# A retention decoder on one core: 32x32 block turns and small transfers in place of transposes on TensorE

## The chip, the cores and the metric

The kernel runs on one core of one Trainium2 chip. The metric is the device time of one execution in microseconds (us), as the median of several runs; lower is better. The profile is of one execution.

## The reference, cut to what matters

One decoder layer over 272 tokens (16 learned meta tokens ahead of 256) with 2048 channels. One input projection of width 22,528 feeds a conformer branch (gated linear unit, causal depthwise convolution of 31 taps, layer norm) and a retention branch of 8 heads; two gates merge them, an output projection and a final norm follow.

```python
qf = rotate_pairs(q, cos, sin) * (RET_QK_DIM ** -0.5)
kf = rotate_pairs(k, cos, sin)
o = retention_chunkwise(qf, kf, v)          # per head: (q k^T * decay) v, 256 x 512 out
o = head_groupnorm(o, ret_gn_w[l], ret_gn_b[l])
y_b = (o * jax.nn.silu(ret_gate)) @ ret_out[l]
merged = jax.nn.sigmoid(merge_a) * y_a + jax.nn.sigmoid(merge_b) * y_b
h_res = h_res + merged @ w_out[l]
```

All data is float32.

## The kernel before, in words

The weights are streamed as chunks of 1 MB (128 x 2048 float32). `seq` is the list of chunks with the work of each; the loop at L731 goes through it. In step i it issues the load of chunk i+3 on SP's queue (three buffers `raw`), splits chunk i+2 into a high and a low part (`cut`: ACT copies `raw` to `whi` rounded to fp32r, VectorE subtracts to give `wlo`; three buffers of each), runs the functions that `marks` holds for step i, then some convolution taps from the list `bg` (VectorE), then the chunk's matmuls and the copies out of PSUM. Each product is made of three fp32r products, high x high, high x low and low x high. Activations lie with channels on the partitions and tokens along the row (`hn`), so a projected chunk comes out as 128 channels x 272 (`project`, L204) or 256 tokens (`project_wide`, L214).

The source order is not the order on the engines: the framework keeps each engine's instructions in one compiled order, and places an instruction where its operands are expected to be ready; the engines then run that order, each waiting on semaphores.

Chunks of one head, in order (before): 2 gates of the linear unit (`sig_b`), 2 of its values (`glu`, after which the head's convolution taps join `bg`), for every head but the first the 4 output-product chunks of the head before (`ret_out_chunks(h - 1)`), 2 of q, 2 of k, 4 of v (`val` copies each from PSUM to `s["v"]`), 4 of the retention gate. That is 20 chunks a head, 16 for the first.

A head's retention runs at marks, counted from the head's first chunk (for heads 1 to 7; four less for head 0):

- `scores` at 14: k by q products on TensorE, times the decay.
- `values` at 17: the values have channels on the partitions, but the next product needs tokens there. Eight 128x128 transposes on TensorE (L394) write two PSUM banks; ACT and VectorE split them into `vhi`, `vlo`. Four more transposes (L402) turn copies of the last 32 tokens. Copies of rows 0 to 31 (`pe`, `ve`) prepare an edge product.
- `attend` at 19: eleven matmuls of 512 columns; group-norm statistics on VectorE, a power -0.5 on POOL (L103), then ACT writes the normalised output `on` (tokens on the partitions).
- `gated` at 21, which is chunk 1 of the next head: eight transposes on TensorE (L454) turn `on` back to channels on the partitions; ACT applies the group norm's scale and shift into `z`, VectorE multiplies by the gate, and `z` is split into `zhi`, `zlo`, which the output products read from chunk 4 of the next head.

The pool `ret` has one buffer for each tag, so tiles of one tag follow each other in one place: `on`; `vT` (the values, then `z`); `zhi`; `zlo`.

The last head's output products come behind four chunks of the merge gate; then follow the rest of the merge gate, the conformer's gate and output, and the output projection.

Of the kernel before, what the change touches and what calls it, by code (L numbers as in the profile page):

```python
# [10 lines left out]
F32 = mybir.dt.float32  # L11
# [5 lines left out]
P = 128  # L17
# [3 lines left out]
SEQ = 256  # L21
# [3 lines left out]
HEADS = 8  # L25
# [11 lines left out]
def hybrid_kernel(ctx: ExitStack, tc, xt, xrow, xnat, par, fg, cs, dec, win, cout, rout, wout, out):  # L37
    nc = tc.nc
# [7 lines left out]
    def bank(pool=misc):  # L46
        return pool.tile([P, 512], F32, tag="ps", name="ps")
# [36 lines left out]
    ident = pers.tile([P, P], F32, name="ident")  # L84
# [168 lines left out]
        stream(win[blk], use)  # L253

    bg = []


    ret = None
# [18 lines left out]
    def head(h):  # L277
        s = {}
        st[h] = s

        def sig_b(j):
            def f(acc):
                t = ret.tile([P, L], F32, tag="sgb", name="sgb", bufs=2)
                s["b", j] = t
                nc.vector.tensor_tensor(out=t, in0=acc[:, 0:L], in1=row, op=ALU.mult)
                nc.scalar.activation(out=t, in_=t, func=AF.Sigmoid)
                nc.vector.tensor_tensor(out=t, in0=t, in1=row, op=ALU.mult)
            return f

        def glu(j):  # L290
            def f(acc):
                nc.vector.tensor_tensor(out=u_sb[j][:, PAD:], in0=acc[:, 0:L], in1=s["b", j], op=ALU.mult)
                if j == 1:
                    bg.extend(conv_ops(h))
            return f

        def rot(which, j, n):
            def f(acc):
                t = ret.tile([P, 2, n], F32, tag=f"rt{j}", name=f"rt{j}")
                s[which, j] = t  # L300
                if n == SEQ:
                    x = tmp.tile([P, SEQ], F32, tag="sg", name="sg")
                    halves(acc, x)
                    acc = x
                nc.vector.tensor_tensor(out=t, in0=acc[:, 0:n].unsqueeze(1).broadcast_to([P, 2, n]),
                                        in1=cs_sb[:, :, L - n:], op=ALU.mult)
                if j == 1:
                    t0, t1 = s[which, 0], t
                    r = ret.tile([P, 2, n], F32, tag=which + "r", name=which + "r")
                    nc.vector.tensor_tensor(out=r[:, 0], in0=t0[:, 0], in1=t1[:, 1], op=ALU.subtract)  # L310
                    nc.vector.tensor_tensor(out=r[:, 1], in0=t1[:, 0], in1=t0[:, 1], op=ALU.add)
                    hi = ret.tile([P, 2, n], F32R, tag=which + "hi", name=which + "hi")
                    lo = ret.tile([P, 2, n], F32R, tag=which + "lo", name=which + "lo")
                    split(r, hi, lo)
                    s[which] = (r, hi, lo)
            return f

        def val(j):
            def f(acc):
                if j == 0:  # L320
                    s["v"] = ret.tile([P, 4, L], F32, tag="vT", name="vT")
                nc.scalar.copy(out=s["v"][:, j], in_=acc[:, 0:L])
            return f

        def gate(j):
            def f(acc):
                if j == 0:
                    s["g"] = ret.tile([P, 4, SEQ], F32, tag="gs", name="gs")
                g, t = s["g"][:, j], tmp.tile([P, SEQ], F32, tag="sg", name="sg")
                halves(acc, g)  # L330
                nc.vector.tensor_tensor(out=g, in0=g, in1=row[:, NMETA:], op=ALU.mult)
                nc.scalar.activation(out=t, in_=g, func=AF.Sigmoid)
                nc.vector.tensor_tensor(out=g, in0=g, in1=t, op=ALU.mult)
            return f

        for j in range(2):
            proj_chunk(B0 + 2 * h + j, L, sig_b(j))
        for j in range(2):
            proj_chunk(A0 + 2 * h + j, L, glu(j))
        if h:  # L340
            ret_out_chunks(h - 1)
        for j in range(2):
            proj_chunk(Q0 + 2 * h + j, SEQ, rot("q", j, SEQ))
        for j in range(2):
            proj_chunk(K0 + 2 * h + j, L, rot("k", j, L))
        for j in range(4):
            proj_chunk(V0 + 4 * h + j, L, val(j))
        for j in range(4):
            proj_chunk(R0 + 4 * h + j, SEQ, gate(j))

    def scores(h):
# [32 lines left out]
        nc.scalar.activation(out=ph, in_=p2, func=AF.Copy)  # L384
        nc.vector.tensor_tensor(out=ph[64:96], in0=p2[64:96], in1=ph[64:96].bitcast(F32), op=ALU.subtract)

    def values(h):
        s = st[h]
        v = s["v"]
        s["vn"] = []  # L390
        for j in range(2):
            ps = bank()
            for b in range(4):
                nc.tensor.transpose(ps[:, b * P:(b + 1) * P], v[:, b, j * P:(j + 1) * P], ident)  # L394
            hi = ret.tile([P, DV], F32R, tag=f"vhi{j}", name=f"vhi{j}")
            lo = ret.tile([P, DV], F32R, tag=f"vlo{j}", name=f"vlo{j}")
            split(ps, hi, lo)
            s["vn"].append((hi, lo))
        ps = bank()
        last = last32(ret, v, 4)  # L400
        for b in range(4):
            nc.tensor.transpose(ps[0:96, b * P:(b + 1) * P], last[:, b], ident)  # L402
        v2 = ret.tile([96, DV], F32R, tag="v2", name="v2")
        nc.scalar.activation(out=v2, in_=ps[0:96], func=AF.Copy)
        nc.vector.tensor_tensor(out=v2[32:64], in0=ps[32:64], in1=v2[32:64].bitcast(F32), op=ALU.subtract)
        s["v2"] = v2

        pe = ret.tile([96, P], F32R, tag="qr", name="pe")
        ve = ret.tile([96, DV], F32R, tag="kr", name="ve")
        for n, (a, b) in enumerate(((0, 0), (0, 1), (1, 0))):  # L410
            rows = slice(32 * n, 32 * n + 32)
            nc.scalar.copy(out=pe[rows], in_=s["p"][a][0:32, SEQ:SEQ + P].bitcast(F32))
            nc.scalar.copy(out=ve[rows], in_=s["vn"][1][b][0:32].bitcast(F32))
        s["edge"] = (pe, ve)

    def attend(h):
# [24 lines left out]
        for i in range(2):  # L441
            nc.scalar.activation(out=on[:, i], in_=pss[i], func=AF.Identity, scale=rs[:, i:i + 1],
                                 bias=sh[:, i:i + 1])

    def gated(h):
        s = st[h]
        z = ret.tile([P, 4, SEQ], F32, tag="vT", name="z")
        for pair in range(2):
            ps = bank()
            for b in range(2):  # L450
                for i in range(2):
                    o = b * SEQ + i * P
                    vb = 2 * pair + b
                    nc.tensor.transpose(ps[:, o:o + P], s["on"][:, i, vb * P:(vb + 1) * P], ident)  # L454
            for b in range(2):
                vb = 2 * pair + b
                nc.scalar.activation(out=z[:, vb], in_=ps[:, b * SEQ:(b + 1) * SEQ], func=AF.Identity,
                                     scale=pcol(C_GW, 4 * h + vb), bias=pcol(C_GB, 4 * h + vb))
        nc.vector.tensor_tensor(out=z, in0=z, in1=s["g"], op=ALU.mult)
        hi = ret.tile([P, 4, SEQ], F32R, tag="zhi", name="zhi")  # L460
        lo = ret.tile([P, 4, SEQ], F32R, tag="zlo", name="zlo")
        split(z, hi, lo)
        s["z"] = (hi, lo)

    def ret_out_chunks(h):
        for g in range(4):
            def use(hi, lo, g=g):
                z_hi, z_lo = st[h]["z"]
                hi = hi.rearrange("p (k c) -> p k c", k=4)
                lo = lo.rearrange("p (k c) -> p k c", k=4)  # L470
                for half in range(2):
                    acc = bank(accp)
                    for b in range(2):
                        col = (2 * half + b) * P
                        contract(acc[:, b * SEQ:(b + 1) * SEQ], hi, lo, z_hi, z_lo, range(4), slice(col, col + P))
                    y = yb[:, 4 * g + 2 * half:4 * g + 2 * half + 2]
                    a = acc.rearrange("p (b t) -> p b t", b=2)
                    if h == 0:
                        nc.scalar.copy(out=y, in_=a)
                    else:  # L480
                        nc.vector.tensor_tensor(out=y, in0=a, in1=y, op=ALU.add)
            stream(rout[4 * h + g], use)
# [4 lines left out]
    for h in range(HEADS):  # L487
        base = len(seq)
        head(h)
        ex = 4 if h else 0  # L490
        marks.setdefault(base + 10 + ex, []).append(lambda h=h: scores(h))
        marks.setdefault(base + 13 + ex, []).append(lambda h=h: values(h))
        marks.setdefault(base + 15 + ex, []).append(lambda h=h: attend(h))
        marks.setdefault(base + 17 + ex, []).append(lambda h=h: gated(h))


    fin = {}
# [328 lines left out]
```

## Time and profile before

| | us |
|---|---|
| median of 3 runs (lowest to highest) | 1459.52 (1456.3 to 1460.04) |
| the profiled execution | 1456.36 |
| span of its instructions | 1454.5 |
| TensorE busy (matmuls) | 1439.5 |
| VectorE busy | 1070.4 |
| ACT busy | 688.3 |
| POOL busy | 10.8 |

The span runs from the first to the last instruction; the time of the execution lies 1.9 us above it. Busy time of TensorE counts each matmul from its start to its modelled end, so neighbouring matmuls overlap in it: what one costs in a row of many is read from start to start. The granted TensorE clock is at its full level, 2.4 GHz, over the whole span (0.999 of it). The other engines have idle time, which costs nothing unless TensorE waits for them.

### The profile page before, as it was taken

What the parts mean: (1) busy time and instruction counts of PE and PEld (TensorE: products, weight loads), DVE (VectorE), ACT (ScalarE), POOL (GpSimd) and SP (SyncE); (2) the same over time, 40 slices, a digit from 0 to 9 for tenths busy, and PEclk for the clock granted to TensorE, in tenths of its full rate; (3) what the DMA queues carried; (4) which work ended last, traced back from release to release, by engine and by line L of the source; (5) the groups of instructions that cost most, each with busy time, mean ns of one, the idle gap of its engine ahead of it and who ended that gap; (6) DMA issues with size and microseconds to landing.
All of it is one profiled execution on the core that took longest, in us unless ns stands there. A gap on an engine that the chain in (4) does not pass through costs nothing.

```text
span 1454.5 us, 23167 instructions
## 1 busy us (share of the span) xinstructions
PE 1439.5 (99%) x9808; PEld 1338.5 (92%) x9808; DVE 1070.4 (74%) x1467; ACT 688.3 (47%) x834; POOL 10.8 (1%) x27
## 2 busy tenths in 40 slices
PE   8999999999999999999999999999999999999997
PEld 8999999999999999999999999989888888888886
DVE  5797946985895796698589569767878876666553
ACT  6555445345444534634443553454555654444433
POOL 0000000000000000000000000000000000000000
PEclk9999999999999999999999999999999999999999
DMA  8655554554554545455445545545455555555752
GB/s 328 228 181 175 174 182 160 179 191 145 178 196 157 174 174 184 172 174 178 173 154 198 165 164 175 186 160 177 171 203 177 200 177 198 176 196 180 289 177 84
DMA packets 39527, 265.74 MB, mean 183 GB/s; under 512 B 4448, under 2 KB 4448, under 8 KB 8416
## 3 DMA queue, kind: packets, MB, share of 16 engines
q1 hardware_dynamic: 37776, 258.70, 51.5%
q10 hardware_dynamic: 1584, 5.57, 1.0%
q8 instruction: 77, 1.26, 0.3%
q14 instruction: 26, 0.21, 0.0%
q0 software_dynamic: 64, 0.00, 0.0%
HBM read 262.15 MB, written 2.10 MB: 182 GB/s over the span
## 4 chain that ended last, share of the span: by engine, by line
PE 99%; issue 0%; ACT 0%; DMA 0%; DVE 0%; POOLq 0%; POOL 0%
PE ps L222 29%; PE ps L220 15%; PE ps L208 11%; PE ps L209 11%; PE ps L211 11%; PE ps L237 4%; PE ps L234 4%; PE ps L235 4%; PE ps L614 2%; PE ps L617 2%; PE ps L613 2%; PE ps L454 0%; PE ps L394 0%; PE ps L430 0%; PE ps L429 0%
## 5 line engine op out<-in xcount | busy, mean ns | idle before, releaser
L51 DVE TENSOR_TENSOR wlo<-raw,whi 128x2048 fp32r<-128x2048 f32 (+1 forms) x246 | 549.9, 2236 | 177.8 <-ACT whi L50 151.1
L50 ACT ACTIVATE whi<-raw 128x2048 fp32r<-128x2048 f32 (+1 forms) x246 | 461.0, 1875 | 304.9 <-PE ps L209 125.7
L222 PE MATMUL ps<-hn,whi 128*128 128x512 f32 x1536 | 384.4, 397 | 0.0
L222 PEld LDWEIGHTS ps<-hn,whi 128*128 128x128 f32 x1536 | 285.4, 189 | 59.0
L208 PE MATMUL ps<-hn,whi 128*128 128x272 f32 x1280 | 326.4, 290 | 7.2 <-ACT whi L50 5.3
L209 PE MATMUL ps<-hn,whi 128*128 128x272 f32 x1280 | 324.9, 287 | 0.0
L208 PEld LDWEIGHTS ps<-hn,whi 128*128 128x128 f32 x1280 | 241.1, 188 | 7.5 <-ACT whi L50 5.3
L209 PEld LDWEIGHTS ps<-hn,whi 128*128 128x128 f32 x1280 | 241.2, 188 | 0.9 <-DVE hn L156 0.2
L272 DVE SCALAR_TENSOR_TENSOR c_sb<-u,par_sb,c_sb 128x256 f32<-128x256 f32 x480 | 205.9, 477 | 1.5
L220 PEld LDWEIGHTS ps<-hn,wlo 128*128 128x128 f32 x1536 | 194.8, 189 | 8.9
L220 PE MATMUL ps<-hn,wlo 128*128 128x256 f32 x1536 | 197.1, 282 | 0.0
L211 PE MATMUL ps<-hn,wlo 128*128 128x272 f32 x1280 | 172.9, 287 | 0.0
L227 ACT COPY half<-ps 128x256 f32<-128x256 f32 x112 | 41.7, 372 | 276.4 <-PE ps L222 276.2
L211 PEld LDWEIGHTS ps<-hn,wlo 128*128 128x128 f32 x1280 | 164.6, 188 | 0.0
L234 PE MATMUL ps<-zhi,whi 128*128 128x256 f32 x512 | 125.9, 280 | 0.0
L235 PE MATMUL ps<-zlo,whi 128*128 128x256 f32 x512 | 125.9, 280 | 0.0
L234 PEld LDWEIGHTS ps<-zhi,whi 128*128 128x128 f32 x512 | 96.3, 188 | 0.0
L235 PEld LDWEIGHTS ps<-zlo,whi 128*128 128x128 f32 x512 | 96.2, 188 | 0.0
L237 PE MATMUL ps<-zhi,wlo 128*128 128x256 f32 x512 | 80.9, 280 | 0.0
L237 PEld LDWEIGHTS ps<-zhi,wlo 128*128 128x128 f32 x512 | 69.1, 188 | 0.0
L222 PE MATMUL ps<-s,whi 128*128 128x512 f32 x256 | 64.7, 395 | 0.0
L222 PEld LDWEIGHTS ps<-s,whi 128*128 128x128 f32 x256 | 47.9, 188 | 10.2
(164 smaller groups left out, 1041.5 us busy)
## 6 DMA issues: line engine op xcount, KB each, us to landing
raw<-in_win_dram SPq DMA_DIRECT2D x174, 1024.0 KB, 4.9
raw<-in_rout_dram SPq DMA_DIRECT2D x32, 1024.0 KB, 4.9
raw<-in_cout_dram SPq DMA_DIRECT2D x16, 1024.0 KB, 4.9
raw<-in_wout_dram SPq DMA_DIRECT2D x16, 1024.0 KB, 4.8
dec<-in_dec_dram ACTq DMA_DIRECT2D x8, 264.0 KB, 4.0
raw<-in_win_dram SPq DMA_DIRECT2D x8, 256.0 KB, 6.8
xr<-in_xrow_dram SPq DMA_DIRECT2D x2, 1024.0 KB, 10.2
tail<-in_xnat_dram ACTq DMA_DIRECT2D x1, 2048.0 KB, 8.5
```

The source lines that it names most:

```text
L50: nc.scalar.activation(out=hi, in_=src, func=AF.Copy)
L51: nc.vector.tensor_tensor(out=lo, in0=src, in1=hi.bitcast(F32), op=ALU.subtract)
L208: nc.tensor.matmul(acc[:, 0:L], lhsT=w, rhs=hn_hi[:, k], start=(k == 0), stop=False)
L209: nc.tensor.matmul(acc[:, 0:L], lhsT=w, rhs=hn_lo[:, k], start=False, stop=False)
L211: nc.tensor.matmul(acc[:, 0:L], lhsT=lo[:, k * P:(k + 1) * P], rhs=hn_hi[:, k], start=False, stop=(k == KT - 1))
L220: nc.tensor.matmul(acc[:, 0:SEQ], lhsT=lo[:, j * P:(j + 1) * P], rhs=a[:, j, 0], start=False, stop=False)
L222: nc.tensor.matmul(both, lhsT=hi[:, k * P:(k + 1) * P], rhs=a[:, k], start=(k == 0), stop=(k == KT - 1))
L227: nc.scalar.copy(out=t, in_=acc[:, SEQ:])
L234: nc.tensor.matmul(acc, lhsT=hi[:, k, col], rhs=a_hi[:, k], start=(j == 0), stop=False)
L235: nc.tensor.matmul(acc, lhsT=hi[:, k, col], rhs=a_lo[:, k], start=False, stop=False)
L237: nc.tensor.matmul(acc, lhsT=lo[:, k, col], rhs=a_hi[:, k], start=False, stop=(j == n - 1))
L272: nc.vector.scalar_tensor_tensor(out=c, in0=u[:, t:t + SEQ], scalar=w, in1=c, op0=ALU.mult, op1=ALU.add)
```

## The change

For heads 0 to 6 the transposes of the values and of the retention output leave TensorE. Each becomes two steps. VectorE turns every 32x32 block in place of partitions (`nc.vector.transpose`, two instructions of 128x512 for each). Then sixteen transfers, issued on POOL's queue, carry the blocks between the four groups of 32 partitions: transfer (a, q) reads 32 partitions x 1 KB and writes 32 partitions x 8 runs of 128 B. ACT and VectorE then read the turned data from the tiles `vy` and `oy` instead of from PSUM. The last head stays as it was.

The marks of those heads move: the new `turn_values` stands at 17, `values` at 20 (before 17), `attend` at 21 (before 19), the new `turn_out` at 23, `gated` at 26 (before 21); 20 and more are chunks 0 and more of the next head. The output products of head h-1 move behind q and k of head h, from chunks 4 to 7 to chunks 8 to 11, for every head from 1 on. New tiles share the tags of old ones: the block-turned values `vx` and later `z` take `on`, `vy` takes `zhi`, `ox` takes `vT`, `oy` takes `zlo`.

```diff
     bg = []
+    BY_PE = (HEADS - 1,)
...
-        if h:
-            ret_out_chunks(h - 1)
         for j in range(2):
             proj_chunk(Q0 + 2 * h + j, SEQ, rot("q", j, SEQ))
         for j in range(2):
             proj_chunk(K0 + 2 * h + j, L, rot("k", j, L))
+        if h:
+            ret_out_chunks(h - 1)
...
+    def blocks_moved(src, dst):
+
+        for a in range(4):
+            for q in range(4):
+                nc.gpsimd.dma_start(out=dst(q, a), in_=src(q, a))
+
+    def turn_values(h):
+
+        s = st[h]
+        if h in BY_PE:
+            return
+        x = ret.tile([P, 4, 2, 4, 32], F32, tag="on", name="vx")
+        for j in range(2):
+            nc.vector.transpose(out=x[:, :, j].rearrange("p q b t -> p b q t"),
+                                in_=s["v"][:, :, j * P:(j + 1) * P].rearrange("p b (q t) -> p b q t", q=4))
+        y = s["vy"] = ret.tile([P, 2, 4, P], F32, tag="zhi", name="vy")
+        blocks_moved(lambda q, a: x[32 * a:32 * a + 32, q].rearrange("p j b t -> p (j b) t"),
+                     lambda q, a: y[32 * q:32 * q + 32, :, :, 32 * a:32 * a + 32].rearrange("p j b t -> p (j b) t"))
...
         for j in range(2):
-            ps = bank()
-            for b in range(4):
-                nc.tensor.transpose(ps[:, b * P:(b + 1) * P], v[:, b, j * P:(j + 1) * P], ident)
+            if h in BY_PE:
...
+            else:
+                ps = s["vy"][:, j].rearrange("p b t -> p (b t)")
...
+    def turn_out(h):
+
+        s = st[h]
+        if h in BY_PE:
+            return
+        x = ret.tile([P, 4, 4, 2, 32], F32, tag="vT", name="ox")
+        for i in range(2):
+            nc.vector.transpose(out=x[:, :, :, i].rearrange("p q b t -> p b q t"),
+                                in_=s["on"][:, i].rearrange("p (b q t) -> p b q t", b=4, q=4))
+        y = s["oy"] = ret.tile([P, 4, SEQ], F32, tag="zlo", name="oy")
+        ys = y.rearrange("p b (i t) -> p (b i) t", i=2)
+        blocks_moved(lambda q, a: x[32 * a:32 * a + 32, q].rearrange("p b i t -> p (b i) t"),
+                     lambda q, a: ys[32 * q:32 * q + 32, :, 32 * a:32 * a + 32])
...
-        z = ret.tile([P, 4, SEQ], F32, tag="vT", name="z")
+        z = ret.tile([P, 4, SEQ], F32, tag="vT" if h in BY_PE else "on", name="z")
...
+            else:
+                ps = s["oy"][:, 2 * pair:2 * pair + 2].rearrange("p b t -> p (b t)")
...
-        marks.setdefault(base + 10 + ex, []).append(lambda h=h: scores(h))
-        marks.setdefault(base + 13 + ex, []).append(lambda h=h: values(h))
-        marks.setdefault(base + 15 + ex, []).append(lambda h=h: attend(h))
-        marks.setdefault(base + 17 + ex, []).append(lambda h=h: gated(h))
+        late = h not in BY_PE
+        for at, f in ((10, scores), (13, turn_values), (16 if late else 13, values), (17 if late else 15, attend),
+                      (19, turn_out), (22 if late else 17, gated)):
+            marks.setdefault(base + at + ex, []).append(lambda h=h, f=f: f(h))
```

## Rows read from the trace of the kernel before

**Rows 1.** The page, part 1: busy us (share), instructions, by engine.

```profile
PE 1439.5 (99%) x9808; PEld 1338.5 (92%) x9808; DVE 1070.4 (74%) x1467; ACT 688.3 (47%) x834; POOL 10.8 (1%) x27
```

**Rows 2.** Waits of TensorE, whole run: us in total, times, longest us.

```profile
PE ps L208 <- ACT whi L50: 5.3, 1, 5.3
PE ps L208 <- DVE sgb L285: 1.9, 1, 1.9
```

**Rows 3.** Timeline of TensorE, second head: start us, us, engine, line, instructions.

```profile
214.90 0.40 PE L222 MATMUL ps<-hn,whi 128*128 128x512 f32 x1
215.14 1.03 PE L394 MATMUL ps<-ident,vT 128*128 128x128 f32 x8
216.01 0.60 PE L402 MATMUL ps<-ident,last 128*96 128x128 f32 x4
216.36 3.80 PE L222 MATMUL ps<-hn,whi 128*128 128x512 f32 x15
...
227.74 0.39 PE L429 MATMUL ps<-vhi,phi 128*128 128x512 f32 x1
...
230.29 3.69 PE L222 MATMUL ps<-hn,whi 128*128 128x512 f32 x15
...
235.94 0.28 PE L208 MATMUL ps<-hn,whi 128*128 128x272 f32 x1
236.06 0.29 PE L209 MATMUL ps<-hn,whi 128*128 128x272 f32 x1
...
241.91 1.03 PE L454 MATMUL ps<-ident,on 128*128 128x128 f32 x8
242.71 0.37 PE L208 MATMUL ps<-hn,whi 128*128 128x272 f32 x1
242.92 0.29 PE L209 MATMUL ps<-hn,whi 128*128 128x272 f32 x1
```

**Rows 4.** Groups of instructions by shape: busy us, mean ns of one, idle before.

```profile
L305 DVE TENSOR_TENSOR rt<-sg,cs_sb 128x512 f32<-128x512 f32 x16 | 10.8, 683 | 0.0
L394 PE MATMUL ps<-ident,vT 128*128 128x128 f32 x64 | 8.3, 272 | 0.0
```

**Rows 5.** Timeline of VectorE, second head (in brackets: idle before, releaser).

```profile
215.74 0.42 DVE L228 TENSOR_TENSOR gs<-ps,half 128x256 f32<-128x256 f32 x1 [3.70 <-ACT half L227]
...
247.37 1.23 DVE L51 TENSOR_TENSOR zlo<-z,zhi 128x1024 fp32r<-128x1024 f32 x1 [1.13 <-ACT zhi L50]
```

**Rows 6.** Busy us of each engine in one head's stretch, clock, DMA share, GB/s.

```profile
331.00:454.00 123.00, 123.00 (x915) 118.17 (x914) 94.68 (x134) 56.09 (x65) 0.70 (x1) 1.00 0.51 175
```

**Rows 7.** DMA queues (packets, MB, share): whole run; then 41 to 47 us.

```profile
q1 hardware_dynamic: 37776, 258.70, 51.5%
q0 software_dynamic: 64, 0.00, 0.6%
```

**Rows 8.** POOL's transfers of line 186: duration ns min/median/max, and us to landing.

```profile
L186 POOL DMA_DIRECT2D rcol<-rcol x2: 504/589/674, 41.6 to 42.3; - x2
DMA to landing us min/median/max: 2.8/3.1/3.3
```

**Rows 9.** Timeline of POOL at the start.

```profile
0.74 0.11 POOL L83 MEMSET idle<- 128x16 f32 x1 [0.29 <-POOLq L815]
0.78 0.20 POOL masks.py:197 MEMSET ident<- 128x128 f32 x1
```

**Rows 10.** Timeline of ACT, second head.

```profile
209.69 0.39 ACT L322 COPY vT<-ps 128x272 f32<-128x272 f32 x1
210.11 0.70 ACT L192 COPY last<-vT 128x128 f32<-128x128 f32 x3
...
217.72 1.08 ACT L50 ACTIVATE vhi<-ps 128x512 fp32r<-128x512 f32 x2
...
221.41 0.62 ACT L413 CAST ve<-vlo 32x512 fp32r<-32x512 f32 x1 [1.03 <-DVE vlo L51]
...
234.82 1.45 ACT L442 ACTIVATE on<-ps,sh,rst 128x512 f32<-128x512 f32 x2 [4.39 <-DVE sh L440]
```

More of the change, by code (lines that the diff above doesn't have):

```diff
@@ L391, in values @@
         for j in range(2):
-            ps = bank()
-            for b in range(4):
-                nc.tensor.transpose(ps[:, b * P:(b + 1) * P], v[:, b, j * P:(j + 1) * P], ident)
+            if h in BY_PE:
+                ps = bank()
+                for b in range(4):
+                    nc.tensor.transpose(ps[:, b * P:(b + 1) * P], v[:, b, j * P:(j + 1) * P], ident)
+            else:
+                ps = s["vy"][:, j].rearrange("p b t -> p (b t)")
             hi = ret.tile([P, DV], F32R, tag=f"vhi{j}", name=f"vhi{j}")
@@ L443, in attend @@
                                  bias=sh[:, i:i + 1])
+    def turn_out(h):
[10 more added lines that the diff above has]
+                     lambda q, a: ys[32 * q:32 * q + 32, :, 32 * a:32 * a + 32])
     def gated(h):
         s = st[h]
-        z = ret.tile([P, 4, SEQ], F32, tag="vT", name="z")
+        z = ret.tile([P, 4, SEQ], F32, tag="vT" if h in BY_PE else "on", name="z")
         for pair in range(2):
[L449 to L454, printed above, removed]
+            if h in BY_PE:
+                ps = bank()
+                for b in range(2):
+                    for i in range(2):
+                        o = b * SEQ + i * P
+                        vb = 2 * pair + b
+                        nc.tensor.transpose(ps[:, o:o + P], s["on"][:, i, vb * P:(vb + 1) * P], ident)
+            else:
+                ps = s["oy"][:, 2 * pair:2 * pair + 2].rearrange("p b t -> p (b t)")
             for b in range(2):
```

## The prediction

> **What bounds the kernel now.** I read the engine totals first: TensorE is busy for 1439.5 of 1454.5 us and VectorE for 1070.4 [rows 1]. Matmuls overlap in such a sum, so the second view was who TensorE waited for: 5.3 us and 1.9 us, once each, and nothing else [rows 2]. With no wait to remove, the time changes only by work taken off TensorE, or by a wait put on it. The third view, TensorE's own order in the second head (us from the start), prices the work and shows how much time lies between the steps [rows 3]; the other engines' timelines then show when a value is there.
>
> **What leaves TensorE.** Eight turns of the values run from 215.14 to 216.01, 0.87 us; eight turns of the output from 241.91 to 242.71, 0.80 us [rows 3]. The 272 ns of one turn [rows 4] is its length in the pipe, and sixteen of it would be 4.35 us; starts count. The matmul behind the output's turns takes 0.21 us to the next start (242.71 to 242.92) where the same pair elsewhere takes 0.12 (235.94 to 236.06) [rows 3]; that 0.09 goes too. So 0.87 + 0.80 + 0.09 = 1.76 us a head, and 12.3 us for seven heads. The four turns of the last tokens (216.01 to 216.36) stay.
>
> **What VectorE gets.** Four 32x32-block turns of 128x512 a head. The trace has no such instruction. The nearest row is an elementwise operation on 128x512 at 683 ns [rows 4]; the ends are 0.68 us and, if a turn costs as much as twice the columns, 1.23 us [rows 5]. I take 0.68, so 2.7 us a head (4.9 at the upper end). VectorE works 94.68 us of a 123 us head [rows 6], so 28 us are idle, and the values' turn falls into an idle 3.70 us before 215.74 [rows 5]. It costs TensorE nothing; without that idle time it would delay only the start of the transfers, and I count that below. ACT reads the turned data from another memory at about the same size of operation; that too is nothing beside the gaps in its timeline.
>
> **What the DMA engines get.** 14 turns x 16 transfers x 256 runs of 128 B = 57,344 packets. The only packets of POOL's queue took 0.6% of 16 engines in 6 us, 9 ns each; the large ones move 258.70 MB in 51.5% of 16 x 1454.5 us, 21.6 GB/s an engine, so 128 B add 6 ns [rows 7]. At 15 ns the new packets fill 3.7% of the engines beside 51.5%. Weight loads have three buffers; I cost this at nothing, and the bandwidth is no bound.
>
> **What POOL gets: the number that decides.** POOL issues 16 transfers in a row for each turn. The trace shows two such issues, of 32 runs each: 504 and 674 ns, landing 2.8 to 3.3 us after issue [rows 8]. The new ones have 256 runs. Below, one costs 0.59 us as there; above, if all of that is per run, 8 x 0.59 = 4.7 us. For how POOL's time grows with the amount, the nearest rows are its fills: 0.11 us for 16 columns, 0.20 us for 128 [rows 9], 0.8 ns for each more. By that 224 more runs cost 0.18 us, T = 0.77 us. A descriptor pair is more work than a column, so I take T = 0.8 to 1.1 us and keep both ends.
>
> The Trainium skill, "DMA: Bandwidth & Descriptors", Anatomy of one DMA, says that descriptor generation is small and that many can be emitted before the added cost shows, which is the low end. Its Rules for kernel authors speak against this change: transfers under 64 KB (these have 32 KB) pay mostly overhead, about 2.0 us fixed each. The row disagrees that this overhead adds up: the two transfers of [rows 8] start 0.7 us apart and each lands about 3 us after its own issue, so they overlap. With 2.0 + 0.08 us one after the other the sum below would give about 1625 us.
>
> **How long the transfers may take.** Chunks are counted from the head's first; one over 256 tokens (q, retention gates) is 5.69 us (216.36 to 227.74 is two), one over 272 (conformer, k, v) 5.97 (235.94 to 241.91) [rows 3]. Value chunk 15 is copied out by 210.1 and VectorE is free from 212.0 (215.74 less 3.70) [rows 5, 10]; with two turns POOL starts at 213.4. The new `values` stands at chunk 20: 215.14 + 3 x 5.69 = 232.2. Before, the first split began 2.6 us behind that mark (217.72 against 215.14) and the last edge copy ended 6.9 us behind it, at 222.03 [rows 3, 10]. So the split is due at 234.8 and the edge is ready at 239.1. `attend` now follows one chunk later instead of two: 232.2 + 0.35 + 5.97 = 238.5, and its fourth matmul, the edge, comes 0.7 us later (eleven take 2.55 us), at 239.2. There is no slack behind the landing, but 21.4 us ahead of it: 16 T + 2.5 us (landing without issue) <= 21.4 gives **T <= 1.18 us**.
>
> For the output: before, `on` was ready at 236.27, 8.5 us behind `attend` at 227.74 [rows 3, 10]; now 247.0. Turns take 1.4 us, up to 2.3 more behind a weight subtraction: POOL starts by 250.7. `gated` stands at chunk 26, 270.3, and the products at chunk 28, 282.2. The z chain ended 6.7 us behind its mark (248.60 against 241.91) [rows 3, 5], so landing is due by 275.5: 16 T + 2.5 <= 24.8, T <= 1.39. This is where the later output products matter: four chunks earlier they would stand at 259. POOL's other work, one power a head, is due just before `on`, near 245, between the two bursts.
>
> POOL, VectorE and ACT run in order, so behind a late transfer the first split on ACT holds the copies out of PSUM and the next weight splits; those have two chunks of lead.
>
> **Sum.** With T at 0.8 to 1.1 us all of it is hidden: -12.3 + 0. The profiled execution took 1456.36 us (span 1454.5 plus 1.9 around it), so 1444.1. That is beside the lowest of the three runs (1456.3); their median, 1459.52, is 3.2 us above, so 1447.2. I forecast **1447.5 us**, its own range 1443 to 1451.
>
> **Rivals.**
> 1. *POOL is slower than the window.* T above 1.18 us stalls TensorE at `attend`, 16 x (T - 1.18) a head, and above 1.39 also at the products. For seven heads 112 us per us of T and bound: break-even at T = 1.29 us, slower by 0.3% from 1.33. T = 1.5 gives 36 + 12 - 12 = +36 us, 1495; T = 2 gives +148, 1607; 4.7 gives over 2200. If each transfer waited for the landing of the one before, T would be 3.1 us [rows 8] and the time 1854 us; the two in that row did not wait, so this has 0.03 of the rival's chance. For it: 256 runs are eight times those measured. Against it: the two equal issues differ by 0.17 us, so much of their time is not per run. Chance 0.22.
> 2. *Just late.* Landing fits, but `attend` has lost its spare chunk and the edge is ready 0.1 us before its use: a slip of 0.3 to 2.4 us a head costs 2 to 17 us, 1449 to 1464. For it: that margin. Against it: ACT's copies for the last tokens ran at 210.11, ahead of their mark at 215.14 [rows 3, 10], so the compiled order moves ready work forward, and the splits too can go earlier. Chance 0.18.
> 3. *The split is moved forward too far.* By the same freedom the order can put the split on ACT before the transfers have landed. ACT then stands still. Weight splits lead by two chunks, 11.4 us, less about 4.5 for a split of 2048 columns (twice the 1.23 of 1024 columns, on either engine, less overlap): some 7 us cost nothing, what is beyond costs TensorE in full. 10 us early gives 14 x 3 - 12 = +30, 1490. For it: the order is fixed before the run. Against it: TensorE's row of waits is nearly empty, so the estimates behind the order hold for what the kernel has now. Chance 0.08.
>
> **How the numbers follow.** Forecast 0.52, rivals 0.18, 0.22, 0.08. Runs of this kernel spread 3.7 us, about 0.3%, so 4.4 us is what a measurement can tell from no change. Faster by more: 0.52 and 0.07 of rival 2, 0.59. Within: 0.11. Slower: rivals 1 and 3, 0.30. The range starts at 1441 (1444.1 less the spread) and goes to 1525, where T is 1.63 us; beyond lie the worse half of rival 1 and a little of rival 3, about 0.15.
>
> **What the next profile shows.** Right: TensorE still has no waits, each of seven heads is 1.76 us shorter, 112 turns are gone; POOL's issues take under 1.2 us and `vhi` waits for nothing long. T is the first number to read. Wrong if TensorE waits for `vhi`, `ve` or `zhi`, or for `whi` because ACT waited for a transfer; if a block turn takes over 1.5 us; or if the weight loads land later than before.

## The result, and the profile after

The changed kernel takes 1445.74 us (median of 4 runs, 1444.08 to 1446.99) where the kernel before took 1457.91 (median of 4, 1456.09 to 1460.04): a ratio of 0.992 [0.9908, 0.9932], 12.2 us less. The forecast was 1447.5 us and 12.3 us less. The profiled execution took 1446.72 us, with a span of 1444.9.

The page of the kernel after first: part 1 (engine totals, as [rows 1]), the two DMA queues of part 3 (as [rows 7]) and the new transfers of part 6 (issues, KB each, median us to landing).

```profile
PE 1429.0 (99%) x9696; PEld 1328.0 (92%) x9696; DVE 1087.1 (75%) x1495; ACT 691.7 (48%) x834; POOL 140.1 (10%) x251
...
q1 hardware_dynamic: 37776, 258.70, 52.4%
q0 software_dynamic: 7232, 7.35, 2.7%
...
vy<-vx POOLq DMA_DIRECT2D x112, 32.0 KB, 2.7
oy<-ox POOLq DMA_DIRECT2D x112, 32.0 KB, 4.4
```

TensorE has 112 instructions fewer and is still busy in 99% of the span; VectorE got 28 instructions and 16.7 us; POOL went from 10.8 to 140.1 us. TensorE's waits in the kernel after, as [rows 2] for the one before:

```profile
PE ps L208 <- ACT whi L50: 5.3, 1, 5.3
PE ps L208 <- DVE sgb L286: 1.9, 1, 1.9
PE ps L208 <- ACT hn L155: 1.0, 1, 1.0
```

Nothing that the change added is among them: no `vhi`, `ve` or `zhi` (the 1.0 us for `hn` lies at 7.5 us, ahead of the first head's retention). So the time must show as a shorter head. Once a head POOL computes the power of the group norm, right behind `attend`, and that serves as a mark. POOL's timeline, in the kernel before (second and fourth head) and then in the kernel after (the second head whole, the fourth head's power):

```profile
233.89 0.70 POOL L103 TENSOR_TENSOR rst<-rs,nhalf 128x2 f32<-128x2 f32 x1 [120.95 <-DVE rs L102]
...
479.49 0.70 POOL L103 TENSOR_TENSOR rst<-rs,nhalf 128x2 f32<-128x2 f32 x1 [122.06 <-DVE rs L102]
```

```profile
215.44 9.21 POOL L392 DMA_DIRECT2D vy<-vx  x16 [77.12 <-DVE vx L401]
244.82 0.71 POOL L103 TENSOR_TENSOR rst<-rs,nhalf 128x2 f32<-128x2 f32 x1 [20.16 <-DVE rs L102]
248.25 6.36 POOL L392 DMA_DIRECT2D oy<-ox  x11 [2.72 <-DVE ox L475]
...
257.61 1.16 POOL L392 DMA_DIRECT2D oy<-ox  x2 [0.97 <-DMA oy<-ox]
...
486.69 0.71 POOL L103 TENSOR_TENSOR rst<-rs,nhalf 128x2 f32<-128x2 f32 x1 [20.22 <-DVE rs L102]
```

Two heads took 245.60 us before (479.49 - 233.89) and 241.87 after: 122.80 and 120.94 us a head, 1.86 us shorter where 1.76 was forecast. The sixteen issues of the values take 9.21 us. The view of their source line, with durations in ns (lowest, median, highest), and below it the time to landing in us:

```profile
L392 POOL DMA_DIRECT2D vy<-vx x112: 584/584/612, 97.0 to 828.6; - x112
L392 POOL DMA_DIRECT2D oy<-ox x112: 584/584/619, 127.4 to 863.2; - x112
...
DMA to landing us min/median/max: 1.8/3.8/6.2
```

This is the number that the forecast called the first to read: T is 0.584 us, on the lower bound (0.59), although each transfer has eight times the runs of those in [rows 8]. The block turns, by the views of their lines:

```profile
L401 DVE STREAM_TRANSPOSE vx<-vT x14: 668/688/709, 94.9 to 818.6; 128x512 f32<-128x512 f32 x14
...
L475 DVE STREAM_TRANSPOSE ox<-on x14: 711/712/715, 125.7 to 851.8; 128x512 f32<-128x512 f32 x14
```

They cost what an elementwise operation of the same size costs [rows 4]. What the new order made of it shows in TensorE's and ACT's timelines of the second head, after (answering to [rows 3, 10]):

```profile
233.49 0.60 PE L425 MATMUL ps<-ident,last 128*96 128x128 f32 x4
...
239.92 0.40 PE L452 MATMUL ps<-vhi,phi 128*128 128x512 f32 x1
...
240.62 0.40 PE L456 MATMUL ps<-ve,pe 96*128 96x512 f32 x1
```

```profile
230.57 1.14 ACT L50 ACTIVATE vhi<-vy 128x512 fp32r<-128x512 f32 x2
...
236.69 0.62 ACT L436 CAST ve<-vlo 32x512 fp32r<-32x512 f32 x1
...
263.04 2.08 ACT L497 ACTIVATE z<-oy,par_sb 128x256 f32<-128x256 f32 x4 [1.25 <-DMA oy<-ox]
```

The split `vhi` is 3 us ahead of the chunk at whose mark it stands in the source (that chunk follows the four turns of the last tokens at 233.49), and finds its data landed. The last edge copy ends at 237.31 and is used at 240.62: 3.3 us to spare. `z` is placed so early that ACT waits 1.25 us for the transfers. Over the run, the waits of all engines in the kernel after say so too:

```profile
ACT z L497 <- DMA oy<-ox: 10.6, 7, 2.3
...
POOL oy L392 <- DMA oy<-ox: 10.2, 10, 1.7
```

Both are hidden: TensorE never waits for `zhi`. The second line is POOL's own: in each of the seven output bursts it stops until an earlier transfer has landed, so these bursts take 10.5 to 11.0 us from the first issue to the end of the last, not 9.21. What it stops for is read below, at e5.

### The profile page after: what moved, and what is told of

It is laid out like the page before. It is cut to its first block, busy times and chain, and to the rows that moved or that the text cites. A ratio compares the mean times of both kernels' runs of the same rounds, so it can differ in the third digit from the quotient of the medians.

```text
span 1444.9 us, 23303 instructions
## 1 busy us (share of the span) xinstructions
PE 1429.0 (99%) x9696; PEld 1328.0 (92%) x9696; DVE 1087.1 (75%) x1495; ACT 691.7 (48%) x834; POOL 140.1 (10%) x251
## 3 DMA queue, kind: packets, MB, share of 16 engines
q1 hardware_dynamic: 37776, 258.70, 52.4%
q0 software_dynamic: 7232, 7.35, 2.7%
q8 instruction: 76, 1.25, 0.3%
## 4 chain that ended last, share of the span: by engine, by line
PE 98%; issue 0%; DMA 0%; ACT 0%; DVE 0%; SPq 0%; POOLq 0%; POOL 0%
PE ps L222 29%; PE ps L220 15%; PE ps L208 11%; PE ps L209 11%; PE ps L211 11%; PE ps L237 4%; PE ps L235 4%; PE ps L234 4%; PE ps L654 2%; PE ps L657 2%; PE ps L653 2%; PE ps L452 0%; PE ps L454 0%; PE ps L453 0%; DMA x_sb<-in_xt_dram 0%
## 5 line engine op out<-in xcount | busy, mean ns | idle before, releaser
L50 ACT ACTIVATE whi<-raw 128x2048 fp32r<-128x2048 f32 (+1 forms) x246 | 461.0, 1875 | 294.0 <-PE ps L209 163.7
L222 PE MATMUL ps<-hn,whi 128*128 128x512 f32 x1536 | 381.0, 396 | 0.0
L222 PEld LDWEIGHTS ps<-hn,whi 128*128 128x128 f32 x1536 | 284.7, 189 | 58.8
L220 PEld LDWEIGHTS ps<-hn,wlo 128*128 128x128 f32 x1536 | 194.8, 189 | 8.9
L220 PE MATMUL ps<-hn,wlo 128*128 128x256 f32 x1536 | 197.1, 282 | 0.0
L234 PE MATMUL ps<-zhi,whi 128*128 128x256 f32 x512 | 125.9, 280 | 0.0
L392 POOL DMA_DIRECT2D vy<-vx x112 | 64.5, 584 | 516.7 <-DVE vx L401 462.1
L234 PEld LDWEIGHTS ps<-zhi,whi 128*128 128x128 f32 x512 | 96.2, 188 | 0.0
L392 POOL DMA_DIRECT2D oy<-ox x112 | 64.8, 586 | 31.4 <-DVE ox L475 16.3
```

What stands on the lines that cost most here:

```text
L50: nc.scalar.activation(out=hi, in_=src, func=AF.Copy)
L220: nc.tensor.matmul(acc[:, 0:SEQ], lhsT=lo[:, j * P:(j + 1) * P], rhs=a[:, j, 0], start=False, stop=False)
L222: nc.tensor.matmul(both, lhsT=hi[:, k * P:(k + 1) * P], rhs=a[:, k], start=(k == 0), stop=(k == KT - 1))
L234: nc.tensor.matmul(acc, lhsT=hi[:, k, col], rhs=a_hi[:, k], start=(j == 0), stop=False)
L392: nc.gpsimd.dma_start(out=dst(q, a), in_=src(q, a))
```

## The experiments

The theory: the gain is the work taken off TensorE, slot by slot, and everything else is hidden as long as POOL's bursts fit their windows (A). Rivals: the new order is itself worth time, or costs some; the later marks and later products are what make the transfers fit (C), against a compiled order that puts work where its operands are ready, whatever the marks say (D); and the cost per transfer, which the forecast sized only between bounds. The kernel before, run beside them on the same chip, is in the third column; the last is the difference of the medians.

| | us | before | ratio, 95% | us less or more |
|---|---|---|---|---|
| e1 order only | 1460.57 | 1458.44 | 1.0008 [0.9999, 1.0017] | +2.1 |
| e2 values only | 1451.85 | 1458.44 | 0.9954 [0.9941, 0.9967] | -6.6 |
| e3 output only | 1453.99 | 1458.44 | 0.9969 [0.9958, 0.9979] | -4.5 |
| e4 products at their old place | 1516.81 | 1458.44 | 1.04 [1.0385, 1.0414] | +58.4 |
| e5 transfers halved | 1492.60 | 1457.19 | 1.0246 [1.0232, 1.026] | +35.4 |
| e6 transfers quartered | 1671.35 | 1457.19 | 1.1468 [1.1452, 1.1483] | +214.2 |
| e7 old marks | 1448.55 | 1457.19 | 0.9938 [0.9925, 0.995] | -8.6 |
| e8 last tokens turned too | 1443.09 | 1457.19 | 0.9904 [0.989, 0.9917] | -14.1 |
| e9 all eight heads | 1443.15 | 1457.47 | 0.99 [0.9886, 0.9913] | -14.3 |
| e10 values only, products at their old place | 1450.28 | 1457.47 | 0.995 [0.9938, 0.9963] | -7.2 |
| the change again | 1444.92 | 1457.47 | 0.9908 [0.9893, 0.9923] | -12.6 |
| e8 again | 1442.84 | 1457.47 | 0.9895 [0.9882, 0.9909] | -14.6 |

### e1: the new order with all turns on TensorE

```diff
-    BY_PE = (HEADS - 1,)
+    BY_PE = range(HEADS)
...
-        late = h not in BY_PE
+        late = h < HEADS - 1
```

> All eight heads transposed on TensorE again, but the output products and the marks stay at their later places. Theory A (the gain is only the start-to-start slots of the 112 turns on TensorE, 1.76 us a head): no change against the kernel before, within 2 us. Theory B (part of the gain comes from the later products and marks, which spread the work of ACT and VectorE): a part of the 12 us shows here, 3 us or more.

No difference that can be told from the spread (the interval holds 1). Between its second and fourth head the power on POOL moves from 243.61 to 489.60: 123.0 us a head, against 122.80 before. The new order gives nothing by itself, and the trace shows where it costs a little: in seven heads the edge matmul (L456) starts 0.05 us behind the end of the last edge copy on ACT, in the second head at 239.65, 0.48 us behind the matmul ahead of it, where the kernel before has 0.24. That is a stall too short for the table of waits. With the transposes on TensorE `attend` now follows them by one chunk, and the edge is just late, as rival 2 had it; in the change the edge is 3.3 us early.

### e2 and e3: the values alone, the output alone

```diff
     def turn_out(h):
...
-        if h in BY_PE:
+        if True:
             return
```

That is e2, with the same edit in `gated`, and `z` back in the buffer `vT`; e3 has it in `turn_values` and `values` instead.

> Only the values of seven heads are turned on VectorE and by transfers; the output is transposed on TensorE, at the later marks. Theory A: 7 x 0.87 = 6.1 us faster than before. Theory B: clearly more or less than half of the 12 us; a whole 12 us if one wait, not the slots, was removed.

> Only the output of seven heads is turned on VectorE and by transfers; the values are transposed on TensorE, at the later marks. Theory A: 7 x 0.89 = 6.2 us faster than before, and with the run on values alone it adds up to the whole change. Theory B: the two parts do not add up to the whole.

Each half gains on its own, and 6.6 + 4.5 = 11.1 us is near the 12.2 of the whole. The heads of e2 take 121.81 us and those of e3 122.05 (the same mark: 242.25 to 485.87, 245.42 to 489.52), so 0.99 and 0.75 us less than 122.80; the forecast had 0.87 for the values and 0.80 + 0.09 for the output. The step is right in sum, with 0.12 too little on the one and 0.14 too much on the other. Both runs have the later marks, and e3 has e1's short stall at the edge as well (0.37 us to the edge matmul in the second head, where e2 has 0.23). Against e1's 123.0 they gain 1.19 and 0.95, and the whole change 2.06: the parts add up to within 0.1.

### e4 and e10: output products at their old place

```diff
+        if h:
+            ret_out_chunks(h - 1)
         for j in range(2):
             proj_chunk(Q0 + 2 * h + j, SEQ, rot("q", j, SEQ))
         for j in range(2):
             proj_chunk(K0 + 2 * h + j, L, rot("k", j, L))
-        if h:
-            ret_out_chunks(h - 1)
...
-                      (19, turn_out), (22 if late else 17, gated)):
+                      (19, turn_out), (20 if late else 17, gated)):
```

That is e4; e10 is e2 with the same move and `gated` at 19.

> The whole change, but the output products stand at chunks 4 to 7 of the next head as before (and gated at chunk 4). In the changed kernel z is split by 268.7 us, and chunk 24 of that head would start near 260.5. Theory C (the place in the source decides, the later products carry the change): TensorE waits some 8 us for zhi in each of seven heads, 45 us slower than before. Rival D (the compiled order puts the chunks that are ready, q and k, in front of the products): no wait, and the gain of 12 us stays.

> Only the values turned, output transposed on TensorE at chunk 23, output products at chunks 4 to 7 of the next head as before. Theory A (the later products are needed for the output's transfers alone): z is split about one us behind the start of chunk 24, so between 6 us faster and 1 us slower than before. Rival (the early place of the products costs by itself): near 50 us slower, as with the whole change.

e4 went the expected way, and further. TensorE waited `PE ps L234 <- ACT zhi L50: 51.4, 7, 8.0`. Its timeline in the second head, and then its windows at the same place (us, busy us and count of PE, PEld, DVE, ACT, POOL, granted clock, DMA share, GB/s):

```profile
264.86 2.14 PE L211 MATMUL ps<-hn,wlo 128*128 128x272 f32 x16
274.30 1.22 PE L234 MATMUL ps<-zhi,whi 128*128 128x256 f32 x4 [7.29 <-ACT zhi L50]
...
275.94 0.42 PE L234 MATMUL ps<-zhi,whi 128*128 128x256 f32 x1
276.15 0.42 PE L235 MATMUL ps<-zlo,whi 128*128 128x256 f32 x1
...
280.52 0.28 PE L235 MATMUL ps<-zlo,whi 128*128 128x256 f32 x1
280.64 0.29 PE L234 MATMUL ps<-zhi,whi 128*128 128x256 f32 x1
```

```profile
267.00:274.30 7.30, 0.01 (x1) 0.00 (x1) 5.93 (x10) 3.76 (x7) 0.00 (x0) 0.71 0.58 203
274.30:277.00 2.70, 2.66 (x10) 2.37 (x11) 2.70 (x6) 0.00 (x0) 0.00 (x0) 0.50 0.00 0
277.00:280.50 3.50, 3.50 (x18) 3.50 (x18) 2.47 (x7) 0.00 (x0) 0.00 (x0) 0.52 0.00 0
280.50:284.00 3.50, 3.50 (x32) 3.50 (x31) 3.28 (x8) 1.02 (x1) 0.00 (x0) 1.00 0.02 5
```

The wait costs twice. While TensorE stands still its granted clock falls, and for some 6 us that follow it is at half, 1.2 GHz: matmuls start 0.21 us apart, then 0.12. At half speed 6 us do the work of 3. The other heads have the same with other lengths: over the 8 us behind each of the seven waits the granted clock is 0.79, 0.62, 0.75, 0.63, 0.74, 0.79 and 0.62, which is 16.5 us of full speed lost beside the 51.4 of waiting. The spans agree: 1512.7 - 1443.0 (the change again) = 69.7, of which 18.3 are not waits. My expectation had the wait and not the clock. e10 shows that only the output's transfers need the later products: with the values alone turned, the old place keeps the whole gain (-7.2 us against -6.6).

### e5 and e6: the same bytes in twice and four times as many transfers

```diff
         for a in range(4):
             for q in range(4):
-                nc.gpsimd.dma_start(out=dst(q, a), in_=src(q, a))
+                for c in range(0, 8, 4):
+                    nc.gpsimd.dma_start(out=dst(q, a)[:, c:c + 4], in_=src(q, a)[:, c:c + 4])
```

e6 has `range(0, 8, 2)` and pieces of 2.

> Each of the 224 transfers of the change is split in two of half the runs (32 issues a turn). Theory A (an issue on POOL costs a fixed 0.58 us whatever it moves, and the time before the data is due decides): 32 x 0.58 = 18.7 us a turn; in the changed kernel the values start at 215.4 and are due at 236.3, the output starts at 248.3 and is due at 277, so both still fit: the gain of 12 us stays, at most 0.5 us a head lost at attend. Theory B (POOL's cost goes with the runs): no change in the length of a turn, 9.2 us, and the same gain.

> Each transfer split in four (64 issues a turn). Theory A: 64 x 0.58 = 37.4 us a turn; the values land some 18 us late and the output some 12 us, in each of seven heads: about 210 us slower than before, more if the clock falls in the waits. Theory B (cost by runs): the turn stays 9.2 us and the gain of 12 us stays.

The expectation for e6 held; that for e5 failed: 35 us slower where the gain should have stayed. First the issues, by the view of the transfers' line in e5 and then in e6 (128 and 64 runs a transfer):

```profile
L393 POOL DMA_DIRECT2D vy<-vx x224: 548/548/576, 93.1 to 879.4; - x112
```

```profile
L393 POOL DMA_DIRECT2D vy<-vx x448: 533/533/551, 93.2 to 1050.2; - x150
```

With 584 ns for 256 runs these lie on a line: 0.27 ns a run ((584 - 533) / 192) above 516 ns that do not depend on it. So a transfer's issue is nearly all fixed cost, and two halves cost 1.096 us in place of one transfer's 0.584. By my window (T <= 1.18) that fits. It did not; waits of e5, of TensorE and then of the others:

```profile
PE ps L457 <- ACT ve L437: 26.5, 7, 4.0
```

```profile
ACT z L498 <- DMA oy<-ox: 65.0, 7, 10.1
ACT vhi L50 <- DMA vy<-vx: 54.8, 7, 9.5
```

Seven times TensorE waits for `ve`, the place of rival 2. POOL's and ACT's timelines of the second head show what the window left out:

```profile
218.59 10.80 POOL L393 DMA_DIRECT2D vy<-vx  x20 [70.39 <-issue]
229.84 0.55 POOL L393 DMA_DIRECT2D vy<-vx  x1 [0.44 <-DMA vy<-vx]
231.33 4.32 POOL L393 DMA_DIRECT2D vy<-vx  x8 [0.95 <-DMA vy<-vx]
236.72 1.63 POOL L393 DMA_DIRECT2D vy<-vx  x3 [1.07 <-DMA vy<-vx]
```

```profile
242.31 1.15 ACT L50 ACTIVATE vhi<-vy 128x512 fp32r<-128x512 f32 x2 [7.84 <-DMA vy<-vx]
...
245.03 1.91 ACT L50 ACTIVATE whi<-raw 128x2048 fp32r<-128x2048 f32 x1
...
247.76 0.62 ACT L437 CAST ve<-vlo 32x512 fp32r<-32x512 f32 x1
```

Three terms are missing. After twenty issues POOL stops for the landing of an earlier transfer, three times and 2.5 us in all. The last transfer has landed, and ACT goes on, 4.0 us behind the last issue (238.35 to 242.31) where I took 2.5. And from the split to the end of the last edge copy ACT takes 6.1 us (242.31 to 248.38) where I took 4.3 (234.8 to 239.1): a copy out of PSUM and the split of a weight chunk, which must go on, get in between. That is 2.46 + 1.46 + 1.77 = 5.69 us against a slack of 16 x (1.18 - 1.096) = 1.34: late by 4.35. Smaller differences take back 0.57 (the 32 issues take 17.30 us, not 17.54; POOL begins 3.74 us behind the start of the head's chunk 16, not 3.91; the edge matmul would start 0.16 us later than the forecast had the edge ready), which leaves 3.8, and TensorE waited 3.8 us in this head and up to 4.0 in others. POOL's start is not among the terms. In the profile of the change it lies at 215.44, against 213.4 in the forecast, because the whole head lies later there: the clock fell in the first head of that execution (last section). The change again has the same burst at the forecast's time:

```profile
213.54 9.21 POOL L392 DMA_DIRECT2D vy<-vx  x16 [76.57 <-DVE vx L401]
```

What POOL stops for can be read transfer by transfer. At each of its stops for a landing (10 in the change, 37 in e5) eight transfers are in flight, and the next issue comes 0.28 us behind the landing of the one eight before it, whose semaphore it uses again: the program gives POOL's transfers eight semaphores in turn. So it is not the length of a burst that stops POOL (it happens after 11 to 14 issues in the change, after 8 to 20 in e5) but eight issues taking less time than a landing, 4.4 us against up to 6.3 in e5. No run has another number of semaphores.

The rest of the loss is again not waiting: 1492.0 - 1443.0 = 49.0 us of span, of which waits on `ve` are 26.5 and others that are new 2.1 (`vlo`, `vhi`); the granted clock is 0.986 in the mean.

In e6 a burst takes 34 us of issues alone (64 x 0.533) and fits no window: TensorE waits 87.3 us for `zhi`, 56.7 for `vhi` and 33.1 for `khi`. The last has nothing to do with the transfers themselves: in the first of these waits ACT waits for VectorE's `kr`, and VectorE works off taps and weight splits from 147 to 185 us without idle time. The mean granted clock is 0.935. This is rival 1's mechanism, POOL slower than the window. That 214 us came out where 210 were expected is in part luck: the issues were shorter than 0.58 us, POOL's stops were not in the sum, and the three waits are 177 us and not 210; of 1668.1 - 1443.0 = 225 us of span the other 48 are not these waits.

### e7: the change with the marks of before

```diff
-        for at, f in ((10, scores), (13, turn_values), (16 if late else 13, values), (17 if late else 15, attend),
-                      (19, turn_out), (22 if late else 17, gated)):
+        for at, f in ((10, scores), (13, turn_values), (13, values), (15, attend),
+                      (17, turn_out), (17, gated)):
```

> The change with the products late, but with the marks of values, attend, turn_out and gated as close as before (17, 19, 21, 21). Theory C (TensorE keeps the source's place and waits): attend at chunk 19 finds its edge operand some 3 us late in seven heads, 21 to 35 us lost against the change, 10 to 23 us slower than before. Rival D (the compiled order of TensorE puts ready chunks in front of attend): no wait and the gain of 12 us stays.

Mostly D: no wait came (the largest new one is 0.2 us for `vlo`), and most of the gain stays. TensorE's timeline in e7 shows what the compiled order did:

```profile
229.05 0.73 PE L452 MATMUL ps<-vhi,phi 128*128 128x512 f32 x2
229.62 0.63 PE L222 MATMUL ps<-hn,whi 128*128 128x512 f32 x2
230.09 1.58 PE L220 MATMUL ps<-hn,wlo 128*128 128x256 f32 x12
231.51 0.45 PE L453 MATMUL ps<-vlo,phi 128*128 128x512 f32 x1
```

`attend` (L452 and on) is not at its mark but in the middle of a chunk of the retention gate (L220, L222), where its operands were expected. So the later marks for `values` and `attend` were not needed to keep TensorE from long waits. -8.6 us is less than the change's -12.2. The trace places 2.0 of those 3.6 us: the power on POOL moves from 235.15 to 477.60 in two heads, 121.22 us a head against 120.94 in the change, and `attend`, cut up by the other chunk, takes longer from start to start (229.05 to 233.76 less the 1.89 of the two L222 and L220 groups, 2.82 us; in a row, before, 2.55). The rest the runs do not place, and the two intervals overlap. Nor do the runs say why in e4 the same freedom did not put a ready chunk ahead of the waiting products.

### e8: the last 32 tokens turned by blocks too

The four turns of the last tokens stay on TensorE in the change. e8 takes them off in seven heads, with one more block turn and 12 small transfers.

```diff
+        xl = ret.tile([P, 4, 32], F32, tag="rt1", name="xl")
+        nc.vector.transpose(out=xl, in_=s["v"][:, :, LAST:L])
+        yl = s["yl"] = ret.tile([96, 4, P], F32, tag="dec", name="yl")
+        for n in range(3):
+            for q in range(4):
+                nc.gpsimd.dma_start(out=yl[32 * n:32 * n + 32, :, 32 * q:32 * q + 32], in_=xl[32 * q:32 * q + 32])
...
-        ps = bank()
-        last = last32(ret, v, 4)
-        for b in range(4):
-            nc.tensor.transpose(ps[0:96, b * P:(b + 1) * P], last[:, b], ident)
+        if h in BY_PE:
...
+        else:
+            ps = s["yl"].rearrange("p b t -> p (b t)")
```

> The whole change, and the four remaining transposes of the last 32 tokens in seven heads go the same way: one more block turn and 12 more transfers in each turn of the values (28 issues, 16.4 us, which fit in the 21 us before they are due). Theory A (start-to-start slots alone): 7 x 0.35 = 2.5 us faster than the change, 14.6 us faster than before. Rival: the longer burst makes attend wait, and it is no faster than the change.

> The changed kernel again, on the chip and in the rounds of the two kernels that turn more: 12 us faster than before.

> The kernel with the last tokens turned in seven heads again: by slots 2.5 us faster than the changed kernel of the same rounds; by the rival (a longer burst on POOL) not faster.

-14.1 us, and -14.6 in a second batch beside the change's -12.6: 2.1 us below it there, where four turns of 0.35 us in seven heads are 2.5. The sign is the same in both batches, but the intervals of the ratios overlap (0.9895 [0.9882, 0.9909] and 0.9908 [0.9893, 0.9923]), so e8 beats the kernel before for certain and the change only probably. TensorE has two short waits in it that the change has not, for `v` and `ve`, 1.8 us together in e8 and 0.9 in e8 again.

### e9: the last head turned as well

```diff
-    BY_PE = (HEADS - 1,)
+    BY_PE = ()
...
-    for d in range(4):
+    for d in range(8):
         proj_chunk(MB0 + d, SEQ, merge_b_store(d))
```

On top of e8, with eight merge-gate chunks ahead of the last head's products to give the transfers their time, and the layer norm's marks moved to fit.

> The change with the last tokens turned as well, and for all eight heads; for the last head eight chunks of the merge gate, not four, stand ahead of its output products, and the layer norm's sums lie closer to their use. Theory A (slots alone): 2.1 us faster than the kernel with the last tokens turned in seven heads, 16 us faster than before. Rival: the closer layer norm or the last head makes TensorE wait, and it is no faster than that kernel.

-14.3 us, no more than e8. The turns of one more head, 1.76 + 0.35 us, did not show. TensorE has two waits for `ve` of 2.0 us together and one for `v` of 0.6, 0.8 to 1.7 us more than in e8 and 1.4 of it in the last head, which is near that size; that they cancelled the gain was not tried. The runs cannot tell e8 and e9 apart.

## Why the prediction was right

**TensorE's slots.** 1.76 us a head was forecast, start to start; 1.86 was measured. The 272 ns of one turn, sixteen times, would have given 30 us; e2 and e3 show that starts were right to count. That the whole came out to 0.1 us (12.3 forecast, 12.2 measured) is in part luck: seven heads of 1.86 are 13.0 us, and the runs of one kernel spread over 3 to 4 us.

**Everything else hidden.** VectorE: 0.69 and 0.71 us a turn, taken as 0.68. DMA: 2.7% of the engines, forecast 3.7, but by other numbers: the queue has 7,168 new packets, 32 a transfer, not 57,344, at 86 ns each (2.7% of 16 x 1444.9 us over 7,232 packets) rather than 15. A packet here is not a run of 128 B. The weight queue's share went from 51.5 to 52.4% and TensorE's wait for `whi` stayed at 5.3 us.

**T was mis-sized, to the safe side.** Taken as 0.8 to 1.1 us, it is 0.584. POOL's fills, which served for the growth, were the wrong neighbour: 0.8 ns for each more of a fill's columns against 0.27 ns a run in e5 and e6. That a run is more work than a column was taken without a row, and it came out the other way. What the forecast's rival 1 feared, cost that grows with the runs, is the one thing that hardly exists; what it did not ask is the number of transfers, which is what e5 and e6 made decide.

The Trainium skill, "DMA: Bandwidth & Descriptors", Anatomy of one DMA, says that many descriptors can be emitted before the cost shows. The trace agrees, with 51 ns for 192 more runs. Its Rules for kernel authors, that transfers under 64 KB are mostly overhead, agree in part: 516 of 584 ns on POOL are fixed, but the landings overlap, 16 issues in 9.21 us with 3.8 us each to landing.

**The windows.** The forecast gave the values' burst until 234.8 us; with T as it is, its last issue ended at 224.65, and the margin of 0.1 us at the edge became 3.3, because ACT's split moved ahead of its mark, as the argument against rival 2 had it. But e5 shows that the formula 16 T + 2.5 was too generous: at 1.096 us it says that the transfers fit, and the kernel was 35 us slower than the one before. It lacked POOL's own waits for landings, 1.5 us of landing and 1.8 us in ACT's order between the split and the last edge copy. The forecast was right here because T was small, not because the window was right. e5 is not T = 1.1 itself: sixteen issues of 1.1 us would put eight in 8.8 us, longer than any landing in these runs (at most 6.7 us, in e6), so POOL should not stop. With e5's other terms TensorE would still have waited some 1.6 us a head (1.46 + 1.77 less 1.28 of slack and 0.33 of the smaller differences); that is an estimate, and no run shows it.

**The later products.** Needed, for the output's transfers alone (e4 and e10), and for a larger price than waits show.

**The rivals.** 1 did not occur; e6 is what it looks like. 2 did not occur in the change; e5 shows it, and e1 and e3 by a fraction of a us. 3 occurred in small: the order placed `z` ahead of the landing in all seven heads, 10.6 us of waiting on ACT, all within the lead that the forecast gave (about 7 us a head).

## What to carry to other kernels

When one engine has no waits, price what leaves it by starts in its own timeline, and what arrives elsewhere by the window until its first use. For a burst of small transfers count transfers, not bytes or runs, and put into the window the issues, the stops for earlier landings (here with eight in flight), the last landing and what the consumer's engine has in its queue behind it. Price a stall of TensorE of several us above its length, since the clock can fall with it. And compare times within a head only between profiles whose heads begin at the same time.

## What the runs showed of the hardware

- POOL's issue of a transfer takes 0.516 us + 0.27 ns a run (64, 128 and 256 runs); with eight transfers in flight, on eight semaphores in turn, it stops until the oldest of them has landed (the change and e5).
- A block turn of 128x512 float32 takes 0.69 to 0.71 us, and one of 128x128 0.27 us (e8).
- Over the 8 us behind waits of 7 to 8 us TensorE's mean granted clock is 0.62 to 0.79 (e4); behind one of 7.29 us it is at its lower level, 1.2 GHz, for some 6 us. After a short one it may or may not fall. In the first head, windows of 48 to 52 and 52 to 56 us, of the change and then of the change again:

```profile
48.00:52.00 4.00, 2.06 (x13) 1.87 (x12) 2.79 (x6) 3.00 (x5) 0.00 (x0) 0.86 0.92 328
52.00:56.00 4.00, 4.00 (x25) 4.00 (x25) 4.00 (x7) 2.81 (x3) 0.00 (x0) 0.71 0.31 79
```

```profile
48.00:52.00 4.00, 2.06 (x17) 1.92 (x16) 3.17 (x6) 3.12 (x5) 0.00 (x0) 1.00 0.75 299
52.00:56.00 4.00, 4.00 (x35) 4.00 (x34) 4.00 (x8) 3.04 (x4) 0.00 (x0) 1.00 0.44 121
```

TensorE is idle for the same 1.94 us in both; in the first the granted clock then falls to 0.86 and 0.71, in the second it stays at 1.00. The spans are 1444.9 and 1443.0 us, and the first head's power on POOL comes at 123.91 and 122.01, so the 1.9 us between these two executions come from this place. What decides it stays open.
